# Mixed gather and dense expert layer: where forty gather pairs, the spread weights' loads and the one-hots are done

## The chip, the cores and the metric

One core of a Trainium2 chip runs the whole program as one launch. The metric is the device time of a launch in microseconds, median of the runs.

## What is computed

The reference is a block with neighbourhood attention, a gated linear recurrence and a retrieval feed-forward layer, followed by a second network of two layers (convolution or banded attention, memory attention, gated feed-forward). The change works in the retrieval layer (PEER) of the first block, and on the vectors of its modulation. Every one of 512 tokens picks 16 of 16384 experts for each of 8 heads, by two top-16 lists of 128 keys whose sums are sorted again:

```python
s1, i1 = lax.top_k(s[:, :, 0], PEER_TOPK)
s2, i2 = lax.top_k(s[:, :, 1], PEER_TOPK)
cand = (s1[..., :, None] + s2[..., None, :]).reshape(PEER_BLOCK, PEER_HEADS, PEER_TOPK * PEER_TOPK)
cidx = (i1[..., :, None] * PEER_NKEYS + i2[..., None, :]).reshape(...)
top, pos = lax.top_k(cand, PEER_TOPK)
idx = jnp.take_along_axis(cidx, pos, axis=-1)
g = jax.nn.softmax(top, axis=-1)
a = jax.nn.gelu(jnp.einsum('tpkd,td->tpk', u[idx], t), approximate=False)
return jnp.einsum('tpk,tpkd->td', (g * a), v[idx])
```

## The kernel before, in words

The first block's mixer comes first, then the retrieval layer (`peer`), then the second network. All matmuls take float32 values split in two parts (`split`, lines 132 and 134, and `weights`, lines 147 and 148): ScalarE (ACT) rounds a tile to its high part, VectorE (DVE) subtracts to get the low part, and TensorE (PE) multiplies high by high, high by low and low by high.

In the retrieval layer the 512 tokens are four tiles of 128. Tile 0 is done by gathers: 128 rows of U and 128 rows of V are fetched per token, one indirect DMA of 128 rows of 4 KB for each, issued by GpSimd (POOL). A U row set is multiplied with the token and summed (line 1155), a V row set is scaled and added to an accumulator `accg` (line 1160), both on DVE. `gathered` hands out these jobs in pairs, five buffers deep (`GBUFS`), three loads ahead. Tiles 1 to 3 are done densely: all 128 x 128 experts, in 128 chunks of 128 experts, for 384 tokens.

**The routing stage.** `peer` weaves three generators on virtual clocks: whichever has the smallest clock goes on, and adds the number that it yields. `route` chooses the experts of the four tiles one after the other (`topk`) and, one tile behind, turns the choices of tiles 1 to 3 into a table of weights in DRAM (`spread`, 32 steps per tile: two one-hot tables on DVE, line 1314, their second one scaled by the softmax weights on ACT, line 1318, four small matmuls on PE, a copy out of PSUM on ACT, line 1331; 16 tokens make one tile `W`, written to `Wd`). `ahead` runs 112 of the 128 hidden chunks (`hidden`: weights U split on ACT, line 1342, and DVE, line 1343, 24 matmuls on PE, Gelu on ACT, result written to `Ad`), then four more. `until_routed` hands out gather pairs. The numbers are `PACE` for a chunk, `GATHER` for a pair, and those in `topk` and `spread`. In this stage PE's order is the written one; the other engines are ordered by the scheduler.

In `topk`, 16 lists are sorted, 50 candidate sums per head and their expert numbers are built in 18 small additions (lines 1255, 1258), the sums are sorted, and the expert numbers at the found positions are read out per head by a compare with 0 to 49, a multiply and a sum over 16 x 50 (lines 1272 to 1275).

**The products stage.** For each expert chunk e, `operands` loads the hidden values (`act` from `Ad`, line 1368), multiplies them with the chunk's weights (line 1372) and splits them, and loads and splits V (line 1375); `products` does 18 matmuls of 512 columns. The weights of 8 chunks at a time are one load `Wr` from `Wd` of 1.5 MB in runs of 512 bytes (line 1365), two buffers, issued at the first chunk of its group. The last 12 chunks do their hidden part here. All these loads are on SP's queue. The gather pairs that are left are handed out evenly until e = 119:

```python
left = self.gather_left
want = left * min(e + 1, 120) // 120
```

**Rows of the modulation.** `rows_of` makes a vector that lies along partitions into 128 equal rows: eight diagonal tiles on DVE (line 372), eight matmuls with ones on PE, two copies on DVE (line 374). It is called for `gt1` at the end of the recurrence, for `a2` and `sh2` in `rows_natural` at the start of the retrieval layer, and for `gt2` ahead of the products.

## Time and profile before

| | |
|---|---|
| median of 3 runs | 3149.11 us (3146.27 to 3153.18) |
| the profiled execution, its own time | 3142.09 us |
| its span in the profile | 3140.3 us |
| PE, DVE, ACT, POOL busy | 94%, 60%, 40%, 13% of the span |
| DMA | 537.79 MB, mean 171 GB/s |
| mean granted TensorE clock | 0.974 |
| routing stage (first hidden chunk to the last) | about 674 to 1302 us |
| products stage (to its last product) | about 1315 to 2007 us |

The times of the runs are of whole launches; everything else is from the one profiled execution. Busy time of PE is the time in which some matmul was under way; matmuls overlap, so a busy PE need not be at its peak. In the views, L121 is the helper through which nearly all matmuls go, so that PE's work is told apart by the tiles' names: `hh,wl` with 384 columns is a hidden chunk, `go,oh` the spreading, `vh,sh` a product, `dg,ones` a row of the modulation.

### The profile page before, as it was taken

How to read it: one execution, taken by the hardware profiler on the slowest of the kernel's cores; microseconds unless marked ns; L12 is line 12 of the kernel's file. 1: busy time of each engine (PE TensorE's matmuls, PEld its weight loads, DVE VectorE, ACT ScalarE, POOL GpSimd, SP SyncE). 2: the span in 40 equal slices, each digit the busy share in tenths (PEclk: the TensorE clock that was granted, in tenths of full speed). 3: DMA queues.
4: the chain of work that ended last, by engine and by line, in shares of the span. 5: the costliest groups of instructions: out<-in, count | busy, mean ns of one | idle time of the engine just before them, and what ended most of it. 6: DMA issues, size and time to landing. Idle time of an engine off the chain costs nothing.

```text
span 3140.3 us, 42392 instructions
## 1 busy us (share of the span) xinstructions
PE 2951.1 (94%) x16073; PEld 2529.5 (81%) x16073; DVE 1898.6 (60%) x3680; ACT 1268.6 (40%) x2275; POOL 401.1 (13%) x398
## 2 busy tenths in 40 slices
PE   7998999999999999898888888899999999999998
PEld 5887887799899999776676767778888887788887
DVE  5744497549999856678788875544433245543323
ACT  4233463343466778522232323432423234433222
POOL 2100000001111110133344431000000000000000
PEclk9999999999999999999999998999999999999999
DMA  6622202236676776899999995222333322123332
GB/s 250 228 64 72 62 1 81 98 126 202 204 239 218 255 248 225 286 353 358 355 363 360 361 353 201 64 72 94 100 95 94 99 86 65 54 88 94 99 103 81
DMA packets 257166, 537.79 MB, mean 171 GB/s; under 512 B 20161, under 2 KB 135105, under 8 KB 252609
## 3 DMA queue, kind: packets, MB, share of 16 engines
q1 hardware_dynamic: 196512, 345.82, 33.8%
q0 software_dynamic: 36864, 134.23, 12.0%
q10 hardware_dynamic: 23584, 55.03, 4.6%
q8 instruction: 126, 2.06, 0.3%
q14 instruction: 80, 0.65, 0.1%
HBM read 484.93 MB, written 50.08 MB: 170 GB/s over the span
## 4 chain that ended last, share of the span: by engine, by line
PE 56%; DVE 19%; DMA 9%; issue 4%; ACT 1%; POOL 1%; SPq 0%; DVEq 0%; ACTq 0%; POOLq 0%
PE bank L121 54%; DMA act<-Ad 7%; DVE wl L1343 2%; DVE gr L1155 2%; DVE accg L1160 2%; DVE vl L134 2%; DVE sl L134 1%; PE bank L608 1%; DVE act L1372 1%; PE bank L1471 1%; DVE idx L1275 1%; DVE tmp L1233 1%; DVE eq L1272 1%; DVE eq L1274 1%; DVE KX L802 1%
## 5 line engine op out<-in xcount | busy, mean ns | idle before, releaser
L121 PE MATMUL bank<-hh,wl 128*128 128x512 f32 (+2 forms) x2304 | 837.0, 364 | 41.8 <-DVE wl L1343 32.3
L121 PE MATMUL bank<-hh,wh 128*128 128x512 f32 (+2 forms) x2304 | 843.0, 367 | 16.2 <-ACT wh L1342 6.8
L121 PE MATMUL bank<-hl,wh 128*128 128x512 f32 (+2 forms) x2304 | 834.5, 362 | 1.5 <-DVE hl L271 0.8
L148 DVE TENSOR_TENSOR wl<-w,wh 128x1024 fp32r<-128x1024 f32 (+2 forms) x280 | 295.0, 1054 | 644.2 <-ACT wh L147 637.5
L147 ACT ACTIVATE wh<-w 128x1024 fp32r<-128x1024 f32 (+2 forms) x280 | 257.5, 920 | 746.1 <-PE bank L121 604.1
L121 PEld LDWEIGHTS bank<-hh,wl 128*128 128x128 f32 x2304 | 437.9, 190 | 101.0 <-DVE wl L1343 42.6
L121 PEld LDWEIGHTS bank<-hh,wh 128*128 128x128 f32 x2304 | 438.1, 190 | 69.9 <-ACT wh L1342 7.6
L121 PEld LDWEIGHTS bank<-hl,wh 128*128 128x128 f32 x2304 | 438.4, 190 | 48.9 <-DVE hl L532 1.6
L121 PE MATMUL bank<-vh,sh 128*128 128x512 f32 x768 | 248.7, 406 | 45.9 <-ACT sh L132 30.8
L121 PE MATMUL bank<-vl,sh 128*128 128x512 f32 x768 | 249.6, 407 | 19.4 <-DVE vl L134 19.2
L1136 POOL DMA_INDIRECT gr<-in_Un_dram,iu x128 | 170.6, 1333 | 735.7 <-DVE accg L1160 493.2
L121 PE MATMUL bank<-vh,sl 128*128 128x512 f32 x768 | 244.3, 400 | 0.0
L132 ACT ACTIVATE sh<-act 128x384 fp32r<-128x384 f32 x128 | 67.1, 525 | 383.4 <-DVE act L1372 347.3
L121 PEld LDWEIGHTS bank<-vh,sh 128*128 128x128 f32 x768 | 149.2, 196 | 80.6 <-ACT sh L132 33.8
L1343 DVE TENSOR_TENSOR wl<-w,wh 128x1024 fp32r<-128x1024 f32 x128 | 156.1, 1221 | 77.3 <-ACT wh L1342 77.3
L1342 ACT ACTIVATE wh<-w 128x1024 fp32r<-128x1024 f32 x128 | 135.1, 1056 | 163.8 <-PE bank L121 144.0
L121 PEld LDWEIGHTS bank<-vl,sh 128*128 128x128 f32 x768 | 149.1, 196 | 59.5 <-DVE vl L134 28.8
L121 PEld LDWEIGHTS bank<-vh,sl 128*128 128x128 f32 x768 | 150.4, 196 | 32.9 <-DVE sl L134 0.2
L1136 POOL DMA_INDIRECT gr<-in_V_dram,iv x128 | 151.4, 1183 | 172.4 <-DVE gr L1155 105.5
L134 DVE TENSOR_TENSOR vl<-w,vh 128x1024 fp32r<-128x1024 f32 x128 | 156.6, 1223 | 13.4 <-ACT vh L132 13.1
L1160 DVE SCALAR_TENSOR_TENSOR accg<-gr,wt,accg 128x1024 f32<-128x1024 f32 x127 | 162.8, 1282 | 0.2 <-DMA gr<-in_V_dram,iv 0.2
L1155 DVE SCALAR_TENSOR_TENSOR gr<-gr,h 128x1024 f32<-128x1024 f32 x128 | 156.0, 1221 | 2.8 <-DMA gr<-in_Un_dram,iu 2.8
(373 smaller groups left out, 4690.9 us busy)
## 6 DMA issues: line engine op xcount, KB each, us to landing
w<-in_U_dram SPq DMA_DIRECT2D x128, 512.0 KB, 4.6
w<-in_V_dram SPq DMA_DIRECT2D x128, 512.0 KB, 6.9
w<-in_wgu_dram SPq DMA_DIRECT2D x84, 512.0 KB, 3.5
Wd<-W ACTq DMA_DIRECT2D x24, 1024.0 KB, 6.8
Wr<-Wd SPq DMA_DIRECT2D x16, 1536.0 KB, 17.6
w<-in_wdown_dram SPq DMA_DIRECT2D x44, 512.0 KB, 3.6
Ad<-act ACTq DMA_DIRECT2D x116, 192.0 KB, 3.7
act<-Ad SPq DMA_DIRECT2D x116, 192.0 KB, 6.5
```

The source lines that it names most:

```text
L121: return self.nc.tensor.matmul(out, a, b, start=start, stop=stop)
L132: self.nc.scalar.activation(hi, src, AF.Copy)
L134: (low or self.nc.vector).tensor_tensor(out=lo, in0=src, in1=hi, op=OP.subtract)
L147: self.nc.scalar.activation(hi[:, :, :n], w[:, :, :n], AF.Copy)
L148: (self.low or self.nc.vector).tensor_tensor(out=lo[:, :, :n], in0=w[:, :, :n], in1=hi[:, :, :n], op=OP.subtract)
L608: nc.tensor.matmul(o, x[k], y[:, kk, :256], start=k == 0 and i == 0 and t % 2 == 0, stop=k == KC - 1 and i == 2, skip_group_check=True)
L802: nc.vector.tensor_tensor(out=half(KX[:, :, l], d), in0=half(e, d), in1=half(kt, d), op=OP.mult)
L1136: nc.gpsimd.indirect_dma_start(out=t, out_offset=None, in_=table, in_offset=bass.IndirectOffsetOnAxis(ap=idx, axis=0))
L1155: nc.vector.scalar_tensor_tensor(t, t, 1.0, self.h0, op0=OP.mult, op1=OP.mult, accum_out=dots[:, h, k:k + 1])
L1160: nc.vector.scalar_tensor_tensor(acc, t, wt[:, h, k:k + 1], acc, op0=OP.mult, op1=OP.add)
L1342: nc.scalar.activation(uh, w, AF.Copy)
L1343: nc.vector.tensor_tensor(out=ul, in0=w, in1=uh, op=OP.subtract)
```

## The change

Five things are done at once. (1) The load `Wr` of a group is cut in six parts of 256 KB, issued at chunks 2 to 7 of the group before (`spread_rows`, `WLATE`). (2) The four rows of the modulation go through DRAM: a store of the vector (`keep_rows`, in `late_mods` in the mixer) and a load that every partition reads in full (`rows_of`). (3) The candidates are 80 regular ones (16, 7 x 8 and 8) in three additions; a found position is turned into two ranks by a few small operations (`ranks`), and each of the two key numbers is read out among 16 instead of the product among 50, for four heads in one instruction. (4) Of four columns of the second one-hot table, two are built by ACT alone: Square of (row number minus key number), then Relu of weight minus weight times that. (5) `PACE` becomes 2.65 and `GATHER` a number for each routing phase. By the program's own numbers 26 pairs were handed out in the routing stage and 103 were left; now 40 are and 89 are left.

```diff
-PACE = 2.95
+PACE = 2.65
+WLATE = 2
-GATHER = 11.0
+GATHER = (13.0, 13.0, 7.0, 6.0, 4.6)
...
-    def rows_of(self, vec, name, pool):
+    def keep_rows(self, n, vec):
+        self.nc.sync.dma_start(self.Rd[n].rearrange("(k p) -> p k", p=128), vec)
+
+    def rows_of(self, n, name, pool):
         o = pool.tile([128, D], F32, name=name)
...
+        self.nc.sync.dma_start(o, self.Rd[n].partition_broadcast(128))
         return o
...
     def late_mods(self):
+        self.Rd = self.tc.dram_tile([4, D], F32, name="Rd")
...
+            if j in (2, 3, 5):
+                self.keep_rows((2, 3, 5).index(j) + (j > 2), t[:, :, 0])
+            if j == 4:
+                self.a2 = self.gain_of(1, t, 0, "a2")
+                self.keep_rows(1, self.a2)
...
         ar = self.pool("ar")
-        rows = self.rows_of(self.gt2, "gt2r", ar)
+        for i in range(GROUP - WLATE):
+            self.spread_rows(pm, 0, i)
+        rows = self.rows_of(3, "gt2r", ar)
...
             if n % 2:
-                yield GATHER
+                yield GATHER[self.phase]
...
         for t in range(5):
+            self.phase = t
...
+        ab = self.ranks(pq, pos, cand)
+        E = pq.tile([128, 2, 8, 16], F32, name="E", bufs=2)
+        for h in range(0, 8, 4):
+            hs = slice(h, h + 4)
+            for c in range(2):
+                eq = pq.tile([128, 4, 16, 16], F32, name="eq")
+                nc.vector.tensor_tensor(out=eq, in0=io[:, None, None, :16].to_broadcast([128, 4, 16, 16]),
+                                        in1=ab[c][:, hs].unsqueeze(3).to_broadcast([128, 4, 16, 16]), op=OP.is_equal)
+                self.anchor = nc.vector.tensor_tensor(out=eq, in0=eq, op=OP.mult,
+                                                      in1=f1[:, hs, c].unsqueeze(2).to_broadcast([128, 4, 16, 16]))
+                nc.vector.tensor_reduce(E[:, c, hs], eq, axis=AX.X, op=OP.add)
+                yield 3.4
...
+    def ranks(self, pq, pos, room):
+        nc = self.nc
+        row, low, a, t = (room[:, :, i * 16:i * 16 + 16] for i in range(4))
+        for x, s, op in ((row, 3, OP.logical_shift_right), (low, 7, OP.bitwise_and)):
+            i = pq.tile([128, 8, 16], U32, name="ri")
+            nc.vector.tensor_scalar(i, pos, s, None, op0=op)
+            nc.vector.tensor_copy(x, i)
+        nc.vector.scalar_tensor_tensor(t, row, 9.0, low, op0=OP.is_ge, op1=OP.mult)
...
+        return a, row
...
+                self.anchor = nc.vector.tensor_tensor(
+                    out=go[:, :2], in0=io.unsqueeze(1).to_broadcast([128, 2, 128]),
+                    in1=gT[:, 0, 0, c:c + 2].unsqueeze(2).to_broadcast([128, 2, 128]), op=OP.is_equal)
                 for i in range(4):
-                    nc.scalar.activation(go[:, i], go[:, i], AF.Copy, scale=gT[:, c + i:c + i + 1])
+                    w, ne, nw = (gT[:, s, a, c + i:c + i + 1] for s, a in ((0, 1), (1, 0), (1, 1)))
+                    if i < 2:
+                        nc.scalar.activation(go[:, i], go[:, i], AF.Copy, scale=w)
+                    else:
+                        nc.scalar.activation(go[:, i], io, AF.Square, bias=ne)
+                        nc.scalar.activation(go[:, i], go[:, i], AF.Relu, bias=w, scale=nw)
...
-        if e % GROUP == 0:
-            self.Wr = pm.tile([128, TD // WT, GROUP, WT], F32, name="Wr", bufs=2)
-            nc.sync.dma_start(self.Wr, self.Wd[:, :, e:e + GROUP, :].rearrange("b p e t -> p b e t"))
+        n, j = divmod(e, GROUP)
+        if j == 0:
+            self.Wr = self.Wn
...
+        if j >= WLATE and e < 128 - GROUP:
+            self.spread_rows(pm, n + 1, j - WLATE)
...
+    def spread_rows(self, pm, n, i):
+        if i == 0:
+            self.Wn = pm.tile([128, TD // WT, GROUP, WT], F32, name="Wr", bufs=2)
+        m = TD // WT // (GROUP - WLATE)
+        bs = slice(i * m, i * m + m)
+        self.nc.sync.dma_start(self.Wn[:, bs], self.Wd[bs, :, n * GROUP:(n + 1) * GROUP, :].rearrange("b p e t -> p b e t"))
```

Three places show how the instructions move. SP's queue in the products stage, around one load of a group's weights (`w` is V of a chunk, `act` its hidden values). Before:

```order
L1368 DMA act<-Ad 128x384 x2
L1375 DMA w<-in_V_dram 128x1024
L1365 DMA Wr<-Wd 128x24x128
L1368 DMA act<-Ad 128x384
L1375 DMA w<-in_V_dram 128x1024
```

And changed:

```order
L1393 DMA w<-in_V_dram 128x1024
L1405 DMA Wr<-Wd 128x4x128 x3
L1386 DMA act<-Ad 128x384
L1393 DMA w<-in_V_dram 128x1024
L1405 DMA Wr<-Wd 128x4x128
L1386 DMA act<-Ad 128x384
L1405 DMA Wr<-Wd 128x4x128
L1393 DMA w<-in_V_dram 128x1024
L1405 DMA Wr<-Wd 128x4x128
```

One load of 24 blocks ahead of the next hidden values became six loads of 4 blocks, which stand over some three chunks.

ACT in the last tile's spreading (`go` is the second one-hot table, `wh` the high part of U, `act` the Gelu). Before:

```order
L1318 ACTIVATE go<-go,gT 128x128 x3
L1331 COPY W<-bank 128x4x128
L1318 ACTIVATE go<-go,gT 128x128 x4
L1331 COPY W<-bank 128x4x128
L1318 ACTIVATE go<-go,gT 128x128 x4
L1342 ACTIVATE wh<-w 128x1024 x2
```

And changed:

```order
L1360 ACTIVATE wh<-w 128x1024
L1333 ACTIVATE go<-go,gT 128x128 x2
L1335 ACTIVATE go<-io,gT 128x128 x2
L1336 ACTIVATE go<-go,gT 128x128 x2
L1360 ACTIVATE wh<-w 128x1024
L1369 ACTIVATE act<-bank 128x384
L1349 COPY W<-bank 128x4x128
```

A step's four scalings became two scalings, two squares and two Relus; no table load stands between them.

DVE in the same place (`oh` and `go` are the one-hots, `wl` the low part of U, `gr` and `accg` a gather pair). Before:

```order
L1343 TENSOR_TENSOR wl<-w,wh 128x1024
L1314 TENSOR_TENSOR oh<-io,eT 128x512
L1314 TENSOR_TENSOR go<-io,eT 128x512
L1160 SCALAR_TENSOR_TENSOR accg<-gr,wt,accg 128x1024
L1155 SCALAR_TENSOR_TENSOR gr,dots<-gr,h_5526 128x1024
```

And changed:

```order
L1361 TENSOR_TENSOR wl<-w,wh 128x1024 x3
L1324 TENSOR_TENSOR oh<-io,eT 128x512
L1327 TENSOR_TENSOR go<-io,gT 128x256
L1324 TENSOR_TENSOR oh<-io,eT 128x512
L1327 TENSOR_TENSOR go<-io,gT 128x256
L1164 SCALAR_TENSOR_TENSOR accg<-gr,wt,accg 128x1024
L1159 SCALAR_TENSOR_TENSOR gr,dots<-gr,h_5504 128x1024
```

The second one-hot is half as wide, the gather pairs stand closer together, and some low parts of U stand three in a row.

## Rows read from the trace of the kernel before

**Rows 1.** The page's 40 equal slices of the span, 78.5 us each.

```profile
PE   7998999999999999898888888899999999999998
...
DMA  6622202236676776899999995222333322123332
```

**Rows 2.** Busy time (instructions in brackets) of each engine, clock and DMA by stage.

```profile
core 0: us, PE busy (x) PEld busy (x) DVE busy (x) ACT busy (x) POOL busy (x), PEclk, DMA share, GB/s
674.00:843.00 169.00, 158.68 (x942) 153.55 (x941) 156.18 (x580) 66.15 (x93) 18.57 (x15) 1.00 0.58 188
843.00:1180.00 337.00, 326.40 (x2036) 323.74 (x2035) 287.92 (x713) 234.47 (x453) 45.64 (x33) 0.99 0.71 236
1180.00:1302.00 122.00, 116.88 (x723) 111.25 (x721) 72.48 (x96) 93.40 (x200) 10.45 (x8) 1.00 0.67 229
1302.00:1315.00 13.00, 1.20 (x4) 0.93 (x4) 9.14 (x16) 3.90 (x6) 2.96 (x3) 0.63 1.03 392
1315.00:1890.00 575.00, 503.36 (x2066) 403.84 (x2066) 462.39 (x637) 167.49 (x230) 231.50 (x192) 0.93 1.01 356
1900.00:2007.00 107.00, 107.00 (x532) 96.74 (x530) 57.65 (x70) 37.98 (x56) 6.91 (x8) 0.99 0.46 152
```

**Rows 3.** DMA of 1296 to 1890 us: 40 slices, queues, issues (median us to landing).

```profile
DMA  9999999999999999999999999999999999999999
GB/s 351 364 341 363 328 383 370 334 362 362 346 370 349 353 367 316 381 361 354 357 372 370 366 340 360 377 362 352 364 350 373 364 340 362 354 378 318 337 390 312
DMA packets 110993, 211.66 MB, mean 356 GB/s; under 512 B 7120, under 2 KB 71213, under 8 KB 110959
...
q1 hardware_dynamic: 82525, 108.66, 53.6%
q0 software_dynamic: 28002, 101.99, 46.7%
...
w<-in_V_dram SPq DMA_DIRECT2D x115, 512.0 KB, 7.0
Wr<-Wd SPq DMA_DIRECT2D x15, 1536.0 KB, 18.0
act<-Ad SPq DMA_DIRECT2D x116, 192.0 KB, 6.5
gr<-in_V_dram,iv POOLq DMA_INDIRECT x102, 7.5
gr<-in_Un_dram,iu POOLq DMA_INDIRECT x93, 7.4
```

**Rows 4.** Who waited for whom, 1280 to 1930 us: total, times, longest.

```profile
DVE act L1372 <- DMA act<-Ad: 113.8, 18, 8.8
...
PE bank L121 <- DVE dg L372: 12.1, 2, 11.4
```

**Rows 5.** Groups of instructions, 674 to 1302 us: busy, mean ns, idle before.

```profile
L121 PE MATMUL bank<-hh,wl 128*128 128x384 f32 x928 | 316.8, 341 | 25.0 <-DVE wl L1343 24.9
...
L1318 ACT ACTIVATE go<-go,gT 128x128 f32<-128x128 f32 x384 | 124.0, 393 | 40.3 <-DVE go L1314 38.0 <-ACT act L1351 0.4
...
L1314 DVE TENSOR_TENSOR go<-io,eT 128x512 f32<-128x512 f32 x96 | 66.0, 688 | 0.0
...
L1155 DVE SCALAR_TENSOR_TENSOR gr<-gr,h 128x1024 f32<-128x1024 f32 x33 | 40.0, 1222 | 2.8 <-DMA gr<-in_Un_dram,iu 2.8
L1272 DVE TENSOR_TENSOR eq<-io,pf 128x800 f32<-128x800 f32 x32 | 31.6, 986 | 0.1
...
L1160 DVE SCALAR_TENSOR_TENSOR accg<-gr,wt,accg 128x1024 f32<-128x1024 f32 x15 | 19.2, 1281 | 0.0
...
L1255 DVE TENSOR_TENSOR cand<-m 128x16 f32<-128x16 f32 (+5 forms) x32 | 5.3, 198 | 0.0
```

**Rows 6.** All matmuls of the modulation's rows, whole span.

```profile
L121 PE MATMUL bank<-dg,ones 128*128 128x128 f32 x64 | 13.1, 320 | 14.4 <-DVE dg L372 14.1 <-DVE r L214 0.2
```

**Rows 7.** Small DMAs of the whole span: KB each, median us to landing.

```profile
bias<-in_nab_dram SPq DMA_DIRECT2D x32, 128.0 KB, 2.1
...
Ld<-lbm ACTq DMA_DIRECT2D x1, 8.0 KB, 3.2
```

More of the change, by code (lines that the diff above doesn't have):

```diff
@@ L1106, in rows_natural @@
         tmp = self.pool("rn")
-        gain, shift = self.rows_of(a2.unsqueeze(2), "a2r", tmp), self.rows_of(self.sh2, "sh2r", tmp)
+        gain, shift = self.rows_of(1, "a2r", tmp), self.rows_of(2, "sh2r", tmp)
         r = self.rstd(self.ss[:, 0], 1e-6)
@@ L1247, in topk @@
         nc.vector.tensor_copy(f1, i1)
-        nc.vector.tensor_scalar(f1[:, :, 0], f1[:, :, 0], 128.0, None, op0=OP.mult)
-        cand = pq.tile([128, 8, 50], F32, name="cand")
-        cidx = pq.tile([128, 8, 50], F32, name="cidx")
-        for dst, src in ((cand, m1), (cidx, f1)):
-            o = 0
-            for a in range(8):
-                n = 16 // (a + 1)
-                nc.vector.tensor_tensor(out=dst[:, :, o:o + n], in0=src[:, :, 0, a:a + 1].to_broadcast([128, 8, n]),
-                                        in1=src[:, :, 1, :n], op=OP.add)
-                o += n
-            nc.vector.tensor_tensor(out=dst[:, :, o:], in0=src[:, :, 0, 8:],
-                                    in1=src[:, :, 1, 0:1].to_broadcast([128, 8, 8]), op=OP.add)
-        yield 2.7
+        cand = pq.tile([128, 8, 80], F32, name="cand")
+        nc.vector.tensor_tensor(out=cand[:, :, :16], in0=m1[:, :, 0, 0:1].to_broadcast([128, 8, 16]), in1=m1[:, :, 1], op=OP.add)
+        nc.vector.tensor_tensor(out=cand[:, :, 16:72].rearrange("p h (a b) -> p h a b", a=7),
+                                in0=m1[:, :, 0, 1:8].unsqueeze(3).to_broadcast([128, 8, 7, 8]),
+                                in1=m1[:, :, 1, None, :8].to_broadcast([128, 8, 7, 8]), op=OP.add)
+        nc.vector.tensor_tensor(out=cand[:, :, 72:], in0=m1[:, :, 0, 8:],
+                                in1=m1[:, :, 1, 0:1].to_broadcast([128, 8, 8]), op=OP.add)
+        yield 1.2
         top = pq.tile([128, 8, 16], F32, name="top")
@@ L1264, in topk @@
             tmp = pq.tile([128, 128], F32, name="tmp", bufs=2)
-            self.top16(top[:, h], pos[:, h], cand[:, h], tmp[:, :50])
-            yield 0.6
-        pf = pq.tile([128, 8, 16], F32, name="pf")
-        nc.vector.tensor_copy(pf, pos)
-        idx = pq.tile([128, 128], F32, name="idx", bufs=2)
-        for h in range(8):
-            eq = pq.tile([128, 16, 50], F32, name="eq")
-            nc.vector.tensor_tensor(out=eq, in0=io[:, None, :50].to_broadcast([128, 16, 50]),
-                                    in1=pf[:, h].unsqueeze(2).to_broadcast([128, 16, 50]), op=OP.is_equal)
-            self.anchor = nc.vector.tensor_tensor(out=eq, in0=eq, in1=cidx[:, h:h + 1].to_broadcast([128, 16, 50]), op=OP.mult)
-            nc.vector.tensor_reduce(idx[:, h * 16:(h + 1) * 16], eq, axis=AX.X, op=OP.add)
-            yield 2.7
@@ L1287, in topk @@
+        e1, e2 = (E[:, c].rearrange("p h k -> p (h k)") for c in range(2))
         g = pq.tile([128, 8, 16], F32, name="g", bufs=2)
@@ L1295, in topk @@
         return e1, e2, g.rearrange("p h k -> p (h k)")
+    def ranks(self, pq, pos, room):
[6 more added lines that the diff above has]
+        nc.vector.scalar_tensor_tensor(t, row, 9.0, low, op0=OP.is_ge, op1=OP.mult)
+        nc.vector.tensor_scalar(a, row, -1.0, 0.0, op0=OP.add, op1=OP.max)
+        nc.vector.tensor_tensor(out=a, in0=a, in1=t, op=OP.add)
+        nc.vector.tensor_tensor(out=low, in0=low, in1=t, op=OP.subtract)
+        nc.vector.tensor_scalar(row, row, 1.0, 8.0, op0=OP.is_equal, op1=OP.mult)
+        nc.vector.tensor_tensor(out=row, in0=row, in1=low, op=OP.add)
+        return a, row
     def spread(self, pq, t, e1, e2, g, io):
```

47 lines of the change are left out of this document (15 added, 32 removed).

## The prediction

> **What bounds the kernel now.** I read the slices first, then the busy times by stage, then the DMA view of the stage that stood out, then its waits. In the slices [rows 1] the DMA digits are 9 only from slice 17 to slice 24, and there PE drops from 9 to 8. The busy times by stage [rows 2] say what these slices are: from 1315 to 1890 us, in the products stage, the 16 DMA engines are busy 1.01 of the time at 356 GB/s, while PE is busy 503 of 575 us at a granted clock of 0.93, DVE 462 and ACT 167. Ahead of it, in the routing stage (674 to 1302), the DMA share is 0.58 to 0.71 and PE is busy 602 of 628 us; behind it (1900 to 2007) PE is busy throughout and the DMA share is 0.46. So PE sets the pace of the routing stage and of the end, and DMA that of the products. The DMA view [rows 3] shows that this is a matter of work and not of one late load: 9 in all 40 slices, 211.66 MB in 594 us. 46.7% of the engines' time goes to the queue of the gathers, 53.6% to SP's. The wait of 113.8 us of DVE for `act` [rows 4] is how this reaches PE: the hidden values stand behind a 1.5 MB load of weights that lands after 18.0 us [rows 3].
>
> **Gather pairs moved: the main term.** The change hands out 40 pairs while routing instead of 26, so 14 pairs, 28 gathers, leave the saturated stage. 195 gathers (102 and 93) took 46.7% of 594 us, 277 us, or 1.42 us each [rows 3]. 28 x 1.42 = **-39.8 us**. DVE loses 28 x 1.25 us of work there too [rows 5], which is not needed for this: at 462 of 575 us it is not the bound. How far can it go on? From 1315 to 1890 PE has about 2066 matmuls of work for 503 us of busy time at a clock of 0.93 [rows 2], some 470 us at full clock; 575 - 40 = 535 is above that, so DMA stays the bound and the whole 39.8 us count. For them to arrive they must cost nothing where they go. There the DMA share is 0.67 to 0.71 [rows 2]; 39.8 us of transfers over 459 us (843 to 1302) add 0.09.
>
> **Weights in six parts: 0 in the sum.** The bytes and the 512-byte runs are the same, and a saturated set of engines gains nothing from another order. The lateness of `act` shrinks, but something else is late instead: V or a gather. Bounds: a gain if the stage ran at the best rate seen in it (390 GB/s in one slice [rows 3]) instead of 356, (211.66 - 14.7) MB / 390 = 505 us against 553, -48; a loss under the rivals.
>
> The Trainium skill (DMA: Bandwidth & Descriptors, sections on bandwidth and on the anatomy of one DMA) speaks against this part: it asks for transfers of at least 1 MiB and, for DMAs issued by GpSimd, puts a fixed cost of about 2.0 us on each. By that, 80 DMAs more would be an estimated 160 us if each stood alone, and the sum would turn positive. The trace speaks for the opposite here: loads of 192 KB and of 512 KB land after nearly the same time, 6.5 and 7.0 us, while the engines are full [rows 3].
>
> **The row for `gt2`.** 512 KB more in the saturated stage: 0.52 MB / 356 GB/s = **+1.5 us**. What it removes looks like more: PE waits 11.4 us for the first diagonal tile [rows 4], with the DMA share at 1.03 meanwhile [rows 2]. Since the stage ends when its bytes are moved, I count that wait at nothing; the cover is the DMA engines' full queue, and if that were gone it would be worth up to -11.4. The load waits on SP for the last store of a hidden chunk, with the `act` and V loads behind it; for those few us earlier loads keep the engines fed.
>
> **The other three rows.** Their 48 matmul records are three quarters of [rows 6]: 9.8 us busy, which overlap, and of the waits 14.4 - 12.1 = 2.3. That is between 0 and -12; the loads in their place are needed only once PE has long gone on. I take half, **-6 us**. New are four stores of 4 KB in single floats, on SP ahead of the mixer's weights. No row shows one; the nearest is a store of 8 KB in short runs, 3.2 us to landing [rows 7]. So 0 to 4 x 3.2 = 13 us; the weights' ring is four buffers deep, so I take **+2**.
>
> **The routing stage.** PE's matmuls are the same, so only its waits can shrink: 24.9 us for the low part of U on DVE [rows 5]. While DVE was full (156 of 169 us, then 288 of 337 [rows 2]) these waits arose. Per tile the read-out goes from 24 passes of 800 elements at 0.98 us (the compare's row stands for the three [rows 5]) to 12 of 1024, by size 1.26 us: 23.6 to 15.1. The 18 additions of about 0.2 us [rows 5] become 3, the ten operations of `ranks` at that price give back 2, and sorting 80 instead of 50 about 1. That is -8 us a tile, -32 in all. Half the second one-hot saves 96 x 0.34 = 33 us [rows 5]; 28 gather operations at 1.22 to 1.28 us [rows 5] add 35. DVE ends up with 30 us less, and with less in the first two tiles, where no spreading runs yet. Ends 0 and -25; I take **-10**.
>
> ACT pays: 2 instructions more per step, 192 x 0.393 = 75 us [rows 5]. From 843 to 1180 two thirds of them make 234 + 50 = 285 of 337 us [rows 2], still beside PE. In the last tile's spreading they make 93.4 + 25 + about 3 for two more hidden chunks = 121 of 122 us [rows 2]: ACT is then as long as PE, with no slack for PE's own order. Ends 0 (instructions back to back overlap) and +25 (all on the path); I take **+5**.
>
> The Trainium skill (ScalarE: Activation LUTs, rules for kernel authors) says to multiply and do Relu on VectorE and not on ScalarE. Its figure is for bf16; here the row has a DVE compare of four float32 columns at 0.69 us and an ACT column at 0.39 us, so it holds in this trace. By the rule the move costs more engine time than it saves, 75 for 33; by the stage's rows it is paid by the engine with room, save in the last tile.
>
> **The sum.** -39.8 + 1.5 - 6 + 2 - 10 + 5 = -47.3. It is made against the profiled execution's own 3142.1 us, which gives 3094.8. That execution is 7.0 us under the median of the runs, 3149.1, so the median should go to **3101.8 us**. Something within 0.2% (6.3 us) can't be told from no change here. With its terms at their bounds together the forecast reaches from about 3076 to 3145, but not all bounds come at once; its own range is 3080 to 3126.
>
> **The rivals.**
> *The bursts were the loss after all.* If short loads let the engines run at the rate of the best slice, the parts bring up to -48 more: 3054, or about 3070 for half of it. For it: the 18.0 us landing and PE's dropped clock. Against: 9 in every slice. Chance 0.10.
> *Routing gives back.* ACT becomes what PE waits for in the last spreading, all 25 us, and the low parts of U come no earlier, because some now stand three in a row on DVE: -47.3 + 20 + 10 = -17, so 3132. For it: 121 of 122. Chance 0.14.
> *The stage is not moved by bytes.* If its length is set by the chain `act`, weights, split, product for each chunk, which keeps its latency, the gathers were hidden and only the small terms stay: about 3144, no change. Against: DMA at 1.01 of the time. Chance 0.05.
> *Slower: SP's queue becomes the bound.* At the six parts, SP's queue has 22 loads per group instead of 17. Now landing times add up to 115 x 7.0 + 116 x 6.5 + 15 x 18.0 = 1829 us in 594 [rows 3], so three are under way at once. If a part lands like `act`, in 6.5 us, a group's six take 39 us where one took 18.0; at three at once that is 7 us per group, 15 groups, +105 on the queue. It decides once SP's loads, and not the engines, end last, that is with a DMA share below about 0.9 in the stage: -47 + 105, 3207. Against: even the smallest load, 128 KB, lands in 2.1 us when the engines are free [rows 7], and parts are asked for up to six chunks ahead. Chance 0.09.
>
> **How the numbers follow.** Forecast 0.62, the rivals 0.10, 0.14, 0.05 and 0.09. Faster: 0.62 + 0.10 + 0.14 = 0.86; same 0.05; slower 0.09. The range leaves out the last two and part of the first rival: 3062 to 3138.
>
> **What would show it.** Right: 167 gathers in the products stage, the stretch from its first product to the end of the saturation near 535 us, DMA share still near 1.0, no wait for a diagonal tile; `go` on ACT longer, ACT near full in the last spreading, PE's wait for the low part of U at about 15 us. Wrong: a DMA share well below 1 with PE waiting for `act` or V; a stage still 575 us long; or a routing stage longer than 628 us, with PE waiting for `go`.

## The result and the profile after

The changed kernel takes 3271.23 us (median of 4 runs, 3265.27 to 3276.27) beside 3147.69 us of the kernel before in the same comparison: ratio 1.0399, 95% interval 1.0379 to 1.0420, slower by 124 us where 3101.8 us was forecast. Its profiled execution took 3269.59 us with a span of 3267.8 us, 127.5 us more than that of before.

Where the 127.5 us lie follows from three instants in each trace: the split of the first hidden chunk's U on ACT, the first product and the last product on PE. The stretch between the first two is called routing below, the stretch from the first to the last product the products stage.

| | before | after | difference |
|---|---|---|---|
| start to the first hidden chunk | 673.4 | 710.1 | +36.7 |
| to the first product | 643.5 | 690.7 | +47.2 |
| to the last product | 690.4 | 734.1 | +43.7 |
| to the end | 1133.0 | 1133.0 | 0 |

So three stretches lose about 40 us each: the mixer, routing and the products. The slices of the page after, to be read against [rows 1]:

```profile
PE   7799898999988998898787878989999999999998
...
PEclk9879999999999999899989889989999999999999
DMA  6722202336676776699888888413233322123332
GB/s 250 185 62 69 83 8 65 113 111 198 219 242 196 269 252 228 210 356 361 304 300 292 302 294 307 139 45 99 87 97 97 97 84 78 53 84 93 95 103 84
```

In the products, slices 17 to 24 counted from 0, the DMA digit is 9 only twice and then 8 (before, 17 to 23 were all 9): the stage has fewer bytes and is longer. Early on, slice 1 moves 185 GB/s (228 before). The busy times by stage, columns as in [rows 2]; the first three windows are routing, the next two products:

```profile
711.00:881.00 170.00, 161.14 (x953) 155.96 (x952) 156.06 (x611) 75.80 (x123) 19.51 (x15) 0.99 0.58 189
881.00:1188.00 307.00, 280.18 (x1693) 274.98 (x1692) 233.14 (x573) 227.72 (x468) 60.56 (x42) 0.97 0.72 243
1188.00:1399.00 211.00, 180.23 (x1047) 172.26 (x1046) 107.91 (x153) 161.40 (x349) 35.58 (x26) 0.93 0.66 225
1400.00:1500.00 100.00, 90.17 (x370) 69.97 (x370) 78.11 (x109) 31.73 (x45) 43.35 (x30) 0.96 1.02 363
1500.00:2000.00 500.00, 409.68 (x1596) 319.50 (x1595) 347.32 (x473) 132.19 (x185) 178.30 (x134) 0.91 0.89 304
```

The first routing window is as full of PE work as before; in the last one PE is busy 180 of 211 us. From 1500 to 2000 us, in the products, PE is busy 410 of 500 us with no engine and no DMA full (DMA 0.89): something waits on something else in turn. The waits from 1401 to 2135 name it, beside [rows 4]:

```profile
DVE act L1390 <- DMA act<-Ad: 162.0, 65, 6.6
PE bank L122 <- DVE vl L135: 94.5, 43, 6.4
```

DVE waits for hidden values 65 times, 2.5 us each, and PE now waits for `vl`, the low part of V, 94.5 us. Before, from 1317 to 2007:

```profile
PE bank L121 <- DVE vl L134: 19.2, 11, 9.0
```

### The profile page after: what moved, and what is told of

It reads as the page before. It is cut to its first block, busy times and chain, and to the rows that moved or that the text cites. A ratio compares the mean times of both kernels' runs of the same rounds, so it can differ in the third digit from the quotient of the medians.

```text
span 3267.8 us, 42564 instructions
## 1 busy us (share of the span) xinstructions
PE 3000.3 (92%) x16009; PEld 2553.9 (78%) x16009; DVE 1840.2 (56%) x3547; ACT 1336.8 (41%) x2467; POOL 432.5 (13%) x398
## 5 line engine op out<-in xcount | busy, mean ns | idle before, releaser
L122 PE MATMUL bank<-hh,wh 128*128 128x512 f32 (+2 forms) x2304 | 850.1, 370 | 46.6 <-ACT wh L1360 30.7
L122 PE MATMUL bank<-vl,sh 128*128 128x512 f32 x768 | 259.3, 421 | 95.0 <-DVE vl L135 94.5
L1140 POOL DMA_INDIRECT gr<-in_Un_dram,iu x128 | 195.6, 1528 | 838.7 <-DVE accg L1164 645.5
L1140 POOL DMA_INDIRECT gr<-in_V_dram,iv x128 | 158.4, 1238 | 129.0 <-DVE gr L1159 56.2
L1390 DVE TENSOR_TENSOR act<-act,Wr 128x384 f32<-128x384 f32 x128 | 71.2, 557 | 177.9 <-DMA act<-Ad 165.7
```

Of the source, the lines that this page charges most:

```text
L122: return self.nc.tensor.matmul(out, a, b, start=start, stop=stop)
L1140: nc.gpsimd.indirect_dma_start(out=t, out_offset=None, in_=table, in_offset=bass.IndirectOffsetOnAxis(ap=idx, axis=0))
L1390: self.anchor = nc.vector.tensor_tensor(out=a3, in0=a3, in1=self.Wr[:, :, e % GROUP], op=OP.mult)
```

## The experiments

Each run was compared with the kernel before on its chip. The medians of the kernel before lie between 3142.4 and 3148.1 us in these comparisons, so a few us between runs of different comparisons show nothing; instants and stages are from one profiled execution of each run. The table has, from each run's trace, the instant of the first hidden chunk and the two stages of the table above.

| run | median us | first hidden | routing | products |
|---|---|---|---|---|
| e1_one_load | 3265.98 | 703.1 | 697.6 | 732.4 |
| e2_rows_by_pe | 3244.55 | 674.1 | 703.1 | 733.1 |
| e3_onehots_dve | 3207.54 | 704.4 | 638.3 | 732.1 |
| e4_gathers_back | 3226.46 | 702.6 | 711.7 | 677.6 |
| e5_stores_act_queue | 3263.51 | 699.7 | 695.4 | 733.9 |
| e6_pair_each_chunk | 3241.39 | 700.0 | 695.2 | 702.2 |
| e7_act_five | 3246.13 | 701.7 | 691.6 | 708.9 |
| e8_one_column | 3233.81 | 699.0 | 666.0 | 736.1 |
| e9_rows_turned | 3236.36 | 675.0 | 695.1 | 730.1 |
| e10_more_buffers | 3256.49 | 706.7 | 709.4 | 706.2 |
| e11_halves_early | 3222.51 | 702.6 | 655.2 | 730.2 |
| e12_only_gathers | 3203.02 | 679.0 | 659.5 | 733.9 |
| e13_v_first | 3182.66 | 702.5 | 694.9 | 653.7 |
| e14_combined | 3079.67 | 674.7 | 616.3 | 654.2 |
| e15_combined_one_load | 3094.95 | 674.9 | 622.6 | 668.2 |
| e16_gathers_v_first | 3114.03 | 673.4 | 656.0 | 650.9 |
| e17_before_v_first | 3135.16 | 676.4 | 647.2 | 680.0 |
| e18_old_readout | 3082.73 | 674.6 | 624.3 | 647.7 |

### The stores in the mixer

SP's timeline around the first store, in the kernel after (start, duration, line, what is issued):

```profile
87.66 0.33 SPq L330 DMA_DIRECT2D w<-in_wmt_dram  x1
88.79 0.38 SPq L366 DMA_DIRECT2D Rd<-gt  x1
89.93 0.33 SPq L330 DMA_DIRECT2D w<-in_wmt_dram  x1
90.94 0.38 SPq L141 DMA_DIRECT2D w<-in_win_dram  x1
```

The DMA view from 88 to 101 us, 40 slices of 0.3 us:

```profile
DMA  0489599899651312291046141122970070363436
GB/s 0 50 139 151 214 378 391 241 57 131 51 88 63 76 25 25 50 38 25 25 13 50 25 25 13 38 25 38 38 38 13 13 25 13 6 38 13 69 38 101
DMA packets 1288, 0.93 MB, mean 71 GB/s; under 512 B 1060, under 2 KB 1060, under 8 KB 1288
...
w<-in_wmt_dram SPq DMA_DIRECT2D x3, 512.0 KB, 14.8
```

The same stretch in the kernel before:

```profile
DMA packets 1148, 3.27 MB, mean 252 GB/s; under 512 B 96, under 2 KB 96, under 8 KB 1147
...
w<-in_wmt_dram SPq DMA_DIRECT2D x6, 512.0 KB, 4.8
```

After the store some 8 us pass in which little moves (39 GB/s from 91 to 99 us at a DMA share of 0.38, where before it was 300 at 0.93), and the mixer's loads land after 14.8 us instead of 4.8. PE, compared instruction by instruction with before, falls behind in four steps, one behind each store, to 41 us. Three runs ask what a store holds up. The first makes the rows on PE again:

```diff
-    def keep_rows(self, n, vec):
...
+            for q in range(4):
+                dg = pool.tile([128, 128], F32, name="dg", bufs=2)
```

> The change without its part (2): the four rows are again made by PE, no store of single floats in the mixer. Theory (each of the four stores holds back the loads behind it on SP's queue by about 10 us): the four gaps of PE between 90 and 190 us go, 41 us come back, some 7 and 5 us are paid for the rows by PE; the first hidden chunk starts at about 675 us instead of 710, total 3235 to 3250. Rival (the stores cost only their issue, the mixer is late because a2 and its order on DVE moved): first hidden chunk still after 700 us, total 3260 to 3285.

Measured 3244.55 us, first hidden chunk at 674.1, as the theory had it; PE's lag in the mixer is 0.4 us. The row for `gt2` costs again: the first product comes 19.0 us behind the last split of U that precedes it (22.1 in the kernel before, 7.2 with the change).

The second issues the stores on ACT's queue:

```diff
-        self.nc.sync.dma_start(self.Rd[n].rearrange("(k p) -> p k", p=128), vec)
+        self.nc.scalar.dma_start(self.Rd[n].rearrange("(k p) -> p k", p=128), vec)
```

> The change with its four stores of single floats issued on ACT's queue instead of SP's, nothing else. Theory (a store keeps its own queue from going on for some 10 us, and on SP's the mixer's loads stand behind it): the four gaps of PE between 90 and 190 us go, first hidden chunk at about 670 us, total 3230 to 3240. Rival (the 1024 tiny elements hold the 16 DMA engines themselves, whichever queue they come from): the gaps stay, first hidden chunk after 700 us, total 3262 to 3280.

3263.51 us, first hidden chunk at 699.7, as in the other runs with these stores (699.0 to 710.1). The rival holds: SP's loads are late behind a store from ACT's queue as well (39 GB/s from 91 to 99 us here too), and PE falls 31 us behind. The same DMA view of this run:

```profile
q1 hardware_dynamic: 345, 1.16, 52.3%
q10 hardware_dynamic: 1040, 0.00, 4.3%
...
w<-in_wmt_dram SPq DMA_DIRECT2D x4, 512.0 KB, 12.4
...
Rd<-gt ACTq DMA_DIRECT2D x1, 4.0 KB, 12.5
```

This agrees with the Trainium skill (DMA: Bandwidth & Descriptors, section "Issuing engines are not separate DMA queues"), by which transfers of all issuing engines run on the same 16 engines.

The third turns each vector on PE before it is stored:

```diff
-        self.nc.sync.dma_start(self.Rd[n].rearrange("(k p) -> p k", p=128), vec)
...
+        nc.tensor.transpose(b[:KC, :128], vec, self.ident)
+        o = self.g.tile([KC, 128], F32, name="vT")
+        nc.vector.tensor_copy(o, b[:KC, :128])
+        nc.sync.dma_start(self.Rd[n].rearrange("(k p) -> k p", p=128), o)
```

> The change, but each of the four vectors is turned by PE first (one transpose into 8 rows of 128, one copy on DVE), so that its store is 8 runs of 512 bytes instead of 1024 single floats. Theory (the number of tiny elements is what a store costs, and it holds all queues): the gaps of PE between 90 and 190 us go, first hidden chunk at 668 to 676 us instead of 700 to 710, total 3230 to 3242. Rival (a store to DRAM with the loads behind it costs this whatever its form, as part of the round trip): first hidden chunk at 695 us or later, total above 3260.

3236.36 us, first hidden chunk at 675.0, as the theory had it. Against turned vectors the four stores of single floats cost 3271.2 - 3236.4 = 35 us. The store itself in eight runs of 512 bytes does not show: 199 GB/s in the 8 us behind the first one, 210 in the same stretch before, and PE's lag is at most 0.5 us up to 138 us. Turning has a price all the same: PE stands 8.40 us ahead of the last transpose, which starts at 148.90 us, for work of DVE, and then is 7 us behind until the rows for `a2` and `sh2`, which it no longer makes, give that back.

### One-hots on ACT

PE's waits over the whole of routing, 711 to 1399 us, after (before, `wl` held it 24.9 us and `wh` 0.8):

```profile
PE bank L122 <- ACT wh L1360: 30.7, 11, 4.2
PE bank L122 <- DVE wl L1361: 30.5, 31, 5.2
```

One of these waits in the last routing window, first in ACT's timeline, then in PE's:

```profile
1280.29 0.68 ACT L1333 ACTIVATE go<-go,gT 128x128 f32<-128x128 f32 x2
1280.87 0.68 ACT L1335 ACTIVATE go<-io,gT 128x128 f32<-128x128 f32 x2
1281.46 0.87 ACT L1336 ACTIVATE go<-go,gT 128x128 f32<-128x128 f32 x2
1282.23 1.01 ACT L1349 COPY W<-bank 128x512 f32<-128x512 f32 x1
1283.04 1.05 ACT L1360 ACTIVATE wh<-w 128x1024 fp32r<-128x1024 f32 x1
```

```profile
1280.44 0.49 PE L122 MATMUL bank<-go,oh 128*128 128x128 f32 x2 [1.02 <-ACT go L1336]
1284.14 0.69 PE L122 MATMUL bank<-hh,wh 128*128 128x384 f32 x1 [3.21 <-ACT wh L1360]
1284.63 0.52 PE L122 MATMUL bank<-hl,wh 128*128 128x384 f32 x1
...
1290.75 0.34 PE L122 MATMUL bank<-hl,wh 128*128 128x384 f32 x1
```

`wh`, the high part of U, stands behind a step's scaling of `go`, and PE waits 3.21 us for it; then its matmuls take 0.52 instead of 0.34 us for some six us. Three runs change this part. The first lets DVE make the whole second one-hot table again:

```diff
-                    out=go[:, :2], in0=io.unsqueeze(1).to_broadcast([128, 2, 128]),
+                    out=go, in0=io.unsqueeze(1).to_broadcast([128, 4, 128]),
...
-                        nc.scalar.activation(go[:, i], io, AF.Square, bias=ne)
-                        nc.scalar.activation(go[:, i], go[:, i], AF.Relu, bias=w, scale=nw)
```

> The change without its part (4): DVE makes the whole second one-hot table and ACT only scales it. Theory (ACT, with 75 us more work in the spreading, makes the high parts of U late): the routing stage shrinks from 688 to 630 to 645 us, PE's wait for the high part of U there from 31 us to below 5; total 3215 to 3235. Rival (the 28 gather operations and their DMAs that moved into the routing stage made it long): routing stage still 680 or more, total 3260 to 3280.

3207.54 us, 64 less; routing is 638.3 us, as the theory had it, with all moved pairs in it. PE's wait for the high part fell from 30.7 to 9.8 us, less far than expected. The second lets ACT build one column instead of two:

```diff
-                    out=go[:, :2], in0=io.unsqueeze(1).to_broadcast([128, 2, 128]),
+                    out=go[:, :3], in0=io.unsqueeze(1).to_broadcast([128, 3, 128]),
...
-                    if i < 2:
+                    if i < 3:
```

> The change with one column of four, not two, of the second one-hot built by ACT alone: 96 x 0.39 = 38 us more on ACT than when it builds none, instead of 75. Building none gave 3207.5, two 3271. Theory (ACT's place in the order of work counts only where ACT is near full, in the last spreading): less than half of the 64 us, total 3210 to 3230. Rival (every column costs the same, since each go that stands ahead of a high part of U delays it): about half, total 3232 to 3245.

3233.81 us, the rival's "about half": each column costs about the same, 28 and 25 us of routing (638.3, 666.0, 690.7). The third writes the load and the split of U one chunk earlier in the program (`halves` is the first part of `hidden`):

```diff
+        u = self.halves(0)
         for e in range(AHEAD):
-            a = self.hidden(pool, e, mv)
+            cur, u = u, self.halves(e + 1) if e + 1 < AHEAD else None
+            a = self.hidden(pool, e, mv, cur)
```

> The change with the load and the two halves of U written one chunk earlier in the program than the chunk's matmuls; ACT's and DVE's work is the same, only its place in their order moves. Theory (a high part of U is late because it stands behind the scaling of one-hots in ACT's order, not because ACT has too much to do; ACT is busy 465 of 688 us): the routing stage from about 691 to 645 to 665 us, PE's wait for the high part below 10 us; total 3220 to 3245. Rival (ACT's amount of work sets the stage): routing 680 us or more, total 3255 to 3280.

3222.51 us, routing 655.2, PE's wait for the high part 2.3 us, as the theory had it. So with the same work on ACT and DVE its place in their order gave 35 us of routing; leaving out the columns gave 52. These 35 are not all a part of the 52, though: in the combined run below, where ACT builds no column, the early halves still shorten routing, from 638.3 to 616.3 us. With the halves early the columns therefore still cost 655.2 - 616.3 = 39 us. PE's main waits that are left in this run's routing:

```profile
PE bank L122 <- DVE wl L1361: 25.4, 22, 8.1
PE bank L122 <- ACT go L1336: 12.3, 20, 1.2
```

### The products stage

The first run goes back to one load of weights for each group:

```diff
-            self.Wr = self.Wn
+            self.Wr = pm.tile([128, TD // WT, GROUP, WT], F32, name="Wr", bufs=2)
+            nc.sync.dma_start(self.Wr, self.Wd[:, :, e:e + GROUP, :].rearrange("b p e t -> p b e t"))
...
-            self.spread_rows(pm, n + 1, j - WLATE)
```

> The change without its part (1): each group's weights are again one load of 1.5 MB at the group's first chunk. Theory (the parts on SP's queue made the products stage latency-bound): the stage from the first product to the end of the load phase goes from about 630 us to 540 to 570, DMA share there back above 0.95, PE's wait for the low part of V from 94 us to below 30; total 3180 to 3210. Rival (the products stage is held by its chain of hidden value, split and product whichever way the weights come): stage still about 630, total 3260 to 3280.

3265.98 us and a stage of 732.4, as the rival had it: the parts were not the cause. The stage's busy times, and two of its waits:

```profile
1401.00:2133.00 732.00, 625.55 (x2592) 507.97 (x2591) 503.68 (x674) 211.02 (x295) 239.29 (x177) 0.92 0.85 291
```

```profile
DVE act L1389 <- DMA act<-Ad: 177.8, 53, 10.5
PE bank L122 <- DVE vl L135: 91.8, 30, 10.1
```

Next, the spacing numbers of the kernel before:

```diff
-PACE = 2.65
+PACE = 2.95
-GATHER = (13.0, 13.0, 7.0, 6.0, 4.6)
+GATHER = (11.0,) * 5
```

> The change without its part (5): the spacing numbers of the kernel before, 26 pairs while routing. Theory (after the change the products stage is not full of transfers, so gathers cost nothing there, and the routing stage is long because of ACT): routing stage 10 us shorter at most, products stage 0 to 10 us longer, total 3260 to 3285. Rival (the moved gathers are what the routing stage lost by, and they buy nothing): routing stage 640 us, total 3225 to 3240. If the gain of the moved gathers had come all the same, the total would be 3300 to 3315.

3226.46 us, the rival's total for another reason: routing became longer, 711.7 us, and the products stage shorter by 56 us, although 194 gathers are issued behind its first product and not 174. `PACE` goes with the read-out's numbers, so for routing the run is inconclusive; for the products it turned the question round: do fewer gathers make the stage longer? The kernel before with the gathers alone moved:

```diff
-GATHER = 11.0
+GATHER = 7.0
```

> The kernel before with nothing changed but the spacing of the pairs (7.0 instead of 11.0), so that 40 are done while routing. The forecast's main term by itself: 28 gathers fewer in the products stage, 690 - 40 = 650 us, total 3105 to 3120. Theory now (fewer pairs than chunks break the regular order on DVE, PE waits for the low part of V, and the stage gets longer with fewer gathers): products stage 715 to 735 us, routing up to 10 us longer, total 3170 to 3195.

3203.02 us, ratio 1.0185 (1.0160 to 1.0211), and the stage as the theory had it; the total is above its range, since routing grew by 16 us. Behind the first product 168 gathers are issued instead of 198 (174 in the change), and the stage goes from 690 to 734 us, with the waits of after:

```profile
1338.00:2072.00 734.00, 626.21 (x2601) 507.16 (x2600) 495.12 (x663) 206.11 (x289) 232.57 (x171) 0.93 0.83 282
```

```profile
DVE act L1372 <- DMA act<-Ad: 189.0, 57, 9.8
PE bank L121 <- DVE vl L134: 106.8, 41, 7.4
```

DVE's order tells why. Its timeline after:

```profile
1724.01 1.21 DVE L135 TENSOR_TENSOR vl<-w,vh 128x1024 fp32r<-128x1024 f32 x1
1725.14 1.21 DVE L1159 SCALAR_TENSOR_TENSOR gr<-gr,h 128x1024 f32<-128x1024 f32 x1
1726.29 0.07 DVE L1159 DVE_READ_ACCUMULATOR gr<-gr,h 128x1 f32 x1
1729.34 0.56 DVE L1390 TENSOR_TENSOR act<-act,Wr 128x384 f32<-128x384 f32 x1 [2.98 <-issue]
1729.82 0.55 DVE L135 TENSOR_TENSOR sl<-act,sh 128x384 fp32r<-128x384 f32 x1
1730.29 1.28 DVE L1164 SCALAR_TENSOR_TENSOR accg<-gr,wt,accg 128x1024 f32<-128x1024 f32 x1
1731.48 1.22 DVE L135 TENSOR_TENSOR vl<-w,vh 128x1024 fp32r<-128x1024 f32 x1
```

and PE's next wait:

```profile
1732.76 0.73 PE L122 MATMUL bank<-vl,sh 128*128 128x512 f32 x2 [3.09 <-DVE vl L135]
```

Counted from 0, the multiply at 1729.34 is chunk 64's, and the `vl` at 1731.48 behind it chunk 62's. DVE stands 2.98 us for values needed two chunks later (the view names no releaser, but in the trace their load, issued at 1722.92, lands at 1729.26), and PE 3.09 us for V, whose high part ACT had finished at 1719.3. The multiply stands ahead of the `vl` of the chunk before for 9 of 115 chunks in the kernel before, for 89 after, for 108 with the gathers alone moved (counted by start times in the traces). This count alone does not set the price: in e4 it is 99, with a stage of 677.6 us and 62.3 us of waiting for `vl`. How far ahead the multiply stands tells more: it is ahead of the `vl` of two chunks before for no chunk in the kernel before, 21 in e4, 61 with the gathers alone moved and 72 after. DVE's order is set when the program is built. In e12 only the pairs' spacing was changed, so there it turned the order; e4, with nearly as many pairs left as before, shows that something else in the change can turn it too.

Three runs left the order or changed it in part. The first hands out one pair at each chunk:

```diff
-            want = left * min(e + 1, 120) // 120
+            want = min(e + 1, left)
```

> The change, but the 89 pairs that are left are handed out one at each of the first 89 chunks instead of spread over 120. Theory (a chunk without a pair lets DVE's order put the next chunk's multiply ahead of the low part of V; the multiply waits for its load, and PE for V): DVE's order is regular for 89 chunks, PE's wait for the low part of V in the stage from 94 us to below 30, the stage from first to last product from 734 us to 640 to 680; total 3185 to 3220. Rival (the stage is held by the loop of the three buffers of hidden values, in whatever order): PE's waits stay, the stage is 720 us or more, total 3255 to 3280.

3241.39 us, stage 702.2: the direction of the theory, but short of its range. The order is nearly regular (20 of 115), and PE's wait for `vl` goes; one of 80 us for `sh`, the high part of the weighted hidden values, takes its place, with DMA full: busy 1.00 from 1390 to 1870 us. A chunk with its pair moves 1.97 MB, 5.5 us at 357 GB/s; behind them, from 1870 to 2097 us, the DMA share is 0.60. Whether even spacing is the better one once the order is held, no run shows. The second run has more buffers for the hidden values:

```diff
-            a = pm.tile([128, TD], F32, name="act", bufs=3)
+            a = pm.tile([128, TD], F32, name="act", bufs=5)
...
```

> The change with five buffers instead of three for the hidden values in the products stage. Theory of the order (DVE stands at a multiply whose values come late because SP may ask for them only when a low part is done three chunks before): with two more buffers the values are there, DVE's wait for them falls from 166 us to below 60 and the stage from 734 to 640 to 680 us; total 3190 to 3220. Rival (the values come late because the DMA engines or the order of loads on SP's queue let them, not for want of a buffer): the wait and the stage stay within 15 us, total 3255 to 3280.

3246.13 us, stage 708.9, PE's wait for `vl` still 86 us, the order as in the change (89 of 115): 25 us less, where the theory had at least 54 and the rival at most 15. The third has more buffers for both loads:

```diff
-            a = pm.tile([128, TD], F32, name="act", bufs=3)
+            a = pm.tile([128, TD], F32, name="act", bufs=4)
...
-        v = self.st.tile([128, 2, 512], F32, name="w", bufs=WBUFS)
+        v = self.st.tile([128, 2, 512], F32, name="w", bufs=WBUFS) if e % 3 else pm.tile([128, 2, 512], F32, name="vw", bufs=2)
```

> The change with four buffers instead of three for the hidden values and six instead of four for V in the products stage. Five buffers for the hidden values alone gave 709 us there instead of 734, and moved DVE's and ACT's waits to V. Theory (the stage is short of buffers on both loads, its bytes would allow 40 us less than before): 650 to 685 us, DMA share above 0.97, total 3190 to 3225. Rival (DVE's order, not the buffers, keeps the loads from being asked for): 705 us or more, total 3235 to 3280.

3256.49 us, stage 706.2, as the rival had it: more buffers do not get round the order (84 of 115). Now the order itself, in the change and then in the kernel before with the gathers moved. The rule puts a chunk's multiply behind the `vl` of the chunk before, on DVE, and changes nothing else:

```diff
+            if e:
+                es.enter_context(self.after(self.low_v))
             self.anchor = nc.vector.tensor_tensor(out=a3, in0=a3, in1=self.Wr[:, :, e % GROUP], op=OP.mult)
...
         vh, vl = self.split(pm, v, [128, 2, 512], "v", bufs=TAIL + OPS_LAG)
+        self.low_v = self.last_low
```

> The change with one rule more for DVE's order: a chunk's multiply stands behind the low part of V of the chunk before. Theory (what makes the stage longer is that the multiply is put ahead of it and waits there for its load): PE's wait for the low part of V from 94 us to below 40, the products stage from 734 to 655 to 695 us; total 3190 to 3230. Rival (the loads of hidden values are late in any order, and PE then waits for the hidden values' split instead): the stage 715 us or more, total 3250 to 3280.

3182.66 us, 89 less; the stage goes from 734.1 to 653.7 us. In all runs with the rule the traces have no multiply ahead of the `vl` of the chunk before.

> The kernel before with 40 pairs while routing (spacing 7.0), which gave 3203 us, and the low part of V ahead of the next multiply. Theory (moving pairs pays only once the order on DVE is held): products stage from 734 to 655 to 695 us, total 3125 to 3165. Rival (fewer gathers can't shorten the stage, since its loads are late by themselves): 715 us or more, total 3185 to 3210.

3114.03 us, ratio 0.9896 (0.9871 to 0.9922), better than the range; stage 650.9:

```profile
1329.00:1980.00 651.00, 606.07 (x2601) 499.31 (x2600) 496.27 (x663) 207.38 (x288) 239.19 (x171) 0.95 0.91 318
```

```profile
DVE act L1375 <- DMA act<-Ad: 66.7, 16, 7.5
...
PE bank L121 <- DVE vl L134: 12.7, 10, 1.6
```

The rule alone in the kernel before:

> The kernel before with nothing but the rule that the low part of V stands ahead of the next multiply. With it and 40 pairs while routing the products stage took 651 us, without either 690. Theory (the order costs the kernel before only the 19 us that PE waits there for the low part of V; the rest of the 39 us is the bytes of the 28 gathers, 1.42 us each at most): products stage 668 to 692 us, total 3125 to 3150. Rival (the order was the whole loss, and the gathers are hidden once it is held): 645 to 660 us, total 3095 to 3115.

3135.16 us, ratio 0.9969 (0.9954 to 0.9984), stage 680.0, as the theory had it. With the order held the moved gathers bring 680.0 - 650.9 = 29 us of the stage, of which routing takes 9 back (647.2 to 656.0); the totals differ by 21 us. The order by itself brings 10 us of the stage.

### Together

Turned vectors, one-hots on DVE, early halves and the rule, in the change:

> The change with four of the edits together: vectors turned before the store, the second one-hot built by DVE and scaled by ACT, the halves of U one chunk earlier, the low part of V ahead of the next multiply. If each acts on its own stretch: first hidden chunk at 675 us, routing stage 620 to 640, products 655 to 695, the rest 1133 us; total 3085 to 3145. If the order on DVE doesn't hold, products 730 us and total 3160 to 3185.

3079.67 us, ratio 0.9782 (0.9760 to 0.9805): 68 us under the kernel before of that comparison, 192 under the change, and the lowest median here. Routing is 616.3 us, below what was expected. The same with one load of weights for each group:

> The run with the four edits, and the weights again in one load of 1.5 MB a group. Theory (parts or one load make no difference, as in the change itself): within 10 us of that run. Rival (with the order held, a burst of 1.5 MB is what makes the hidden values late): 20 to 45 us more than that run.

3094.95 us: with the order held, the parts are worth 15 us, between the two expectations. They are smaller and also asked for earlier; which of the two counts, no run separates. The combined run with the old read-out of `topk` and its spacing:

> The run with the four edits, with the read-out of the kernel before (50 candidates, one number among 50 for each head) and its spacing of hidden chunks, 2.95, that goes with it. Theory (DVE is full in the first two tiles, and the new read-out takes about 8 us a tile from it): the routing stage 616 us there, 625 to 650 here, total 3088 to 3115. Rival (DVE's relief is hidden behind PE): within 7 us of that run's 3079.7.

3082.73 us, as the rival had it: routing, with three pairs more in it, is 8 us longer, and the products, with three pairs fewer left, are 6.5 us shorter.

## Why the prediction was wrong, step by step

The miss is 169 us, 3271.2 for 3101.8. Three terms carry most of it: the gathers (the products stage +43.7 where -39.8 was counted), the stores (PE's lag of 41 us in the mixer where +2 was counted) and the one-hots on ACT (52 us of routing where +5 was counted). Two of the prediction's own signs of being wrong came true: a DMA share well below 1 with PE waiting for V, and a longer routing stage, though PE waited there for the halves of U more than for `go`.

**Gathers, -39.8.** The failing step is "DMA stays the bound and the whole 39.8 us count". It took DVE's order for fixed. The forecast cleared DVE by its busy time, 462 of 575 us; but in the traces one DVE instruction that waits holds up what stands behind it, and DVE was busy only 495 of 734 us in e12 while PE waited 106.8 us for its `vl`. As made, the move cost 44 us of the stage (e12); with the order held it brought 29 (e17 to e16). The price was too high as well: e16 has 30 gathers fewer in the stage than e17, so each is worth about 1.0 us and not 1.42; and in the change itself 24 gathers left the stage by the traces, not 28. "They must cost nothing where they go" also fell short: routing grew by 16 us in e12, and by 9 with the order held.

**Parts, 0.** Right for the change itself: 3266.0 against 3271.2, ranges overlapping. But the reason given, a saturated set of engines, was gone, and with the order held the parts gain 15 us. By the rule of the Trainium skill weighed there (DMA: Bandwidth & Descriptors, section "Bandwidth", at least 1 MiB for each transfer) they would have lost. The prediction's reading against that rule was weak all the same: that loads of 192 and 512 KB land after nearly the same time is also what a fixed cost of each load would look like, and its fourth rival reads the two rows that way.

**Rows.** The stores were counted at +2 from bounds of 0 to 13, by a store of 8 KB in short runs [rows 7]; they cost 35 us of the total. The wrong step is "the weights' ring is four buffers deep", taken as cover: the loads behind a store came late together (14.8 us to landing for 4.8), and PE fell behind after each of the four. The three rows' -6 held, with some luck in the half that was taken: PE's lag falls from 43.5 to 36.2 us where `a2` and `sh2` were made. The row for `gt2`, +1.5, was mis-signed: the 19.0 us from the last split to the first product (e2) became 7.2, close to the -11.4 named as the other end. The cover, a full DMA queue, did not hold it in this stage, which was no longer saturated.

**ACT, +5 of 0 to 25.** 64 us of the total and 52 of routing, outside the bounds. The step "still beside PE" took ACT's sum, 285 of 337 us, for its effect, and the sign it gave, ACT near full in the last spreading, did not come: ACT is busy 161 of 211 us there. Order is a part of it, as the `wh` behind `go` shows. By e3, e11 and the combined run it is the smaller part: the columns cost 52 us with the halves in their old place and 39 with them early, so some 13 us go to that order. (The combined run differs from e11 by the turned vectors and the rule on `vl` too, but these left routing at 695 us by themselves.) Why the other 39 remain is open; PE's waits for `wl` and `go` in e11 are a part of them. The rule of the Trainium skill that spoke against this part (ScalarE: Activation LUTs, rules for kernel authors) agrees with the runs: 64 us less without it.

**Routing, -10.** No worth of the new read-out is shown: with everything else in place it makes 3 us in the medians of different comparisons, and the intervals of the ratios overlap (0.9760 to 0.9805 with it, 0.9789 to 0.9825 without).

**The rivals.** The mark of "SP's queue becomes the bound" came true, a DMA share of 0.85 in the stage (0.92 before), and its price, 3207, was nearest. Its mechanism, parts on SP's queue, fell with e1, so that is chance. "Routing gives back" named the right engine and wait, at less than half the price. None named DVE's order.

**Sums.** The terms at their bounds give 3074 to 3149 and not 3076 to 3145, and the third rival's small terms 3142 and not 3144; neither bears on the outcome.

Still open: why the build puts the multiply ahead; no run looked into the scheduler.

## What to carry to other kernels

Before work is taken out of a saturated stage, look at the order in which its engines will then run the rest: an instruction that moves ahead of an older one can wait for a load and hold up what others need, on an engine that is far from full. Pin the order of the two instructions that matter, then move work. Store vectors to DRAM in runs of 512 bytes rather than as single floats. And when two edits each shorten a stage, run them together before one is called the cause of the other's gain.

## What was not expected of the hardware

A store of 1024 single floats, 4 KB, brought the DMA engines down to 39 GB/s for some 8 us whichever queue issued it (loads behind it landed after 14.8 and 12.4 us); as eight runs of 512 bytes it did not show. The Trainium skill (DMA: Bandwidth & Descriptors, specifications) says that below 512 bytes the engine reads, modifies and writes; the runs fit that, but don't show the mechanism.

In one place a wait cost PE more than its length. Behind the 3.21 us above, in which PE stood still, the granted clock is 0.51 from 1284.0 to 1290.6 us, the level of 1.2 GHz, with matmuls of 0.52 us; then it is 1.00, the level of 2.4 GHz, and they take 0.34. The mean granted clock is 0.960 after, 0.974 before and 0.983 in the combined run, whose slices show it at full nearly throughout:

```profile
PEclk9999999999999999999999989999999999999999
```
